# A two-layer hybrid block on one core: new orders at five seams, a tail that ends in additions, and first weights by Vector and Scalar's queue

## The chip, the cores and the metric

The kernel runs on one core of one Trainium2 chip. The metric is the time of one execution on the device, in microseconds. A core has a tensor engine (PE in the profile, with its weight loads as PEld), Vector (DVE), Scalar (ACT), GpSimd (POOL) and Sync (SP), which here only starts transfers. Scalar can start transfers as well (its rows are ACTq).

## The reference

A model of depth 2 takes x (512 tokens, width 1024) and a memory of 256 rows. Everything is float32.

```python
for layer in range(DEPTH):
    a = rmsnorm(h, ln_mix_pre[layer])
    mem_n = rmsnorm(mem, ln_mem[layer])
    if layer < N_A_LAYERS:
        proj = a @ w_in_a[layer]                       # u 768, v 768, q_mem 256
        main = chunked_spatial_gating(u, v, ...)       # gelu(u) * (w_s @ layernorm(gelu(v)) + b_s)
    else:
        kvf = rmsnorm(h, ln_shared) @ w_shared_kv      # keys, values, forget gates
        proj = a @ w_in_b[layer - N_A_LAYERS]
        main = forgetting_attention(q, k_s, v_s, log_f_s)   # 12 heads, causal, with decay
    mixed = concatenate([main, memory_attention(q_mem, mem_n, w_mem_kv[layer])])   # 4 memory heads
    h = h + rmsnorm(mixed @ w_out[layer], ln_mix_post[layer])
    f = rmsnorm(h, ln_ffn_pre[layer])
    f = (silu(f @ w_gate) * (f @ w_up)) @ w_down       # hidden width 2816
    h = h + rmsnorm(f, ln_ffn_post[layer])
```

## The kernel before

**Numbers.** Each float32 operand is kept as two parts: `hi`, a rounded copy made by Scalar, and `lo`, the rest, made by Vector (`split`, line 238). A product is three matmuls, hi·hi, hi·lo and lo·hi (`mm3`, line 180). So each weight tile of 128x1024 is loaded by Sync into a `raw` tile (four of them), cast by Scalar, subtracted by Vector, and multiplied by PE.

**Order of the work.** The program is traced in the order of the text, with work placed by hand: `attend` (line 520) runs the heads one after the other in fixed steps and calls pieces of other work (`between`) at five places of each head, so that PE has something to do while a softmax is under way. A last pass, with no new head, finishes the one before. A scheduler then makes each engine's own order, from what it takes each instruction to last and from the place in the text; `behind(x)` makes the instructions of its block come after `x` on the engine of `x`.

**Stages that the change touches.**
- *Start* (`layer_a`, lines 555 to 615). `tokens(k)` loads block k of x (256 KB) on Sync's queue and makes its scaled parts `ahi` (Scalar) and `alo` (Vector); `first_value_weights(n)` and `query_weights(m, half)` load half tiles of weights. `first_values(k)` multiplies four token blocks with the first value weights, three matmuls for each token block in turn. At the very beginning eleven matmuls on zeros (line 85) keep PE busy.
- *End of layer A's memory attention* (lines 710 to 789). Behind the last exponential, Scalar takes the gelu of six value tiles `vg` (line 716). `stats` and `normed` are the layer norm over them, `gate_inputs(m)` makes six gates u, each of 24 matmuls 512 wide, into PSUM tiles of the tag `mm`, which `spatial(g)` uses too (three tiles to a tag).
- *Tail of a projection* (`tail_of`, line 792). `tail(tb)` finishes the product of one token block, adds it to `ys`, takes the sum of squares on Scalar, and scales by r = 1/rms, which GpSimd computes (`rsqrt`, line 251).
- *Boundary* (`boundary`, line 884), three times. PE transposes the scaled token blocks, Vector adds them to the residual h, and the next projection's inputs `xs` are made by quarters (`turn`). The first half of the tokens starts with three token blocks finished; the fourth is still in `tail(3)`. Then r of the new norm is spread over the partitions by PE (`rb`, `spread`), and the sums of the first group are evacuated (`evac`).
- *Feed-forward* (`feed_forward`, line 1063). Products by blocks with seven multiplications in place of eight (`Seven`, line 973), then the down projection by groups of hidden tiles.
- *Layer B* (line 1151). `logarithms` (line 1264) makes the forget gates, with a table load on Scalar.
- *The end* (lines 1373 to 1396). `give` transposes a finished token block back, multiplies by the last gain and adds to h (`residual`, line 850), and stores. For the last block two of the eight tiles go by Scalar and GpSimd, and the last store is on Scalar's queue.

Of the kernel before, what the change touches and what calls it, by code (L numbers as in the profile page):

```python
# [15 lines left out]
P = 128  # L16
T = 512
D = 1024
KT = 8
# [23 lines left out]
def hybrid(ctx: ExitStack, tc: tile.TileContext, i: dict, out: bass.AP):  # L43
# [10 lines left out]
    last_load, last_exp, last_split = [None], [None], [None]  # L54
# [183 lines left out]
    def split(src, hi, lo, eng=None):  # L238
        last_split[0] = A.copy(hi, src), (eng or V).tensor_sub(lo, src, hi)  # L239

    def scaled_parts(src, g, hi, lo):

        A.activation(hi, src, AF.Copy, scale=g)
        V.scalar_tensor_tensor(out=lo, in0=src, scalar=g, in1=hi, op0=ALU.mult, op1=ALU.subtract)
# [174 lines left out]
    class Softmax:  # L419
# [21 lines left out]
        def turn(self, n, pieces):  # L441
# [6 lines left out]
            split(tr[:, :w], hi[:, :w], lo[:, :w])  # L448
            self.tr[n] = hi, lo
# [105 lines left out]
    def layer_a():  # L555
# [5 lines left out]
        def some_weights(raw, src, half, parts, w):  # L561
# [4 lines left out]
            split(raw[:, c], *pair)  # L566
            parts.extend(cut(pair, w))

        def query_weights(m, half):
            some_weights(raws[m], i["w_a_q"][m], half, wq[m], P)  # L570

        def first_value_weights(n):
            some_weights(raws[2 + n // 2], i["w_a_v"][0, n // 2], n % 2, w0, 256)
# [65 lines left out]
        with tc.tile_pool(name="sgu", bufs=1) as lp:  # L639
# [69 lines left out]

            between = {n: take(fill, 3) for n in range(4)}  # L710
            between[1].append(spatial_parts)
            between[3].append(spatial_bias)
            attend(mem_heads(0, q, mixed), between=between)
            with tc.issue_after(last_exp[0].ins):
                for vt in vg.values():
                    A.activation(vt, vt, AF.Gelu_apprx_tanh)
            us, vp = [], {}
            mv = lp.tile([P, TB, 2], F32, name="mv")
            rv = small("rv")

            wu = []

            def gate_inputs(m):
                while len(wu) < min(m + 2, NG):
                    wu.append(prepared(i["w_a_u"][len(wu)], (KT, P)))
                [o] = group([wu[m]], a, FULL, ["mm"])
                us.append(plain("u"))
                V.tensor_mul(us[m], o, rbc)
                A.activation(us[m], us[m], AF.Gelu_apprx_tanh)

            def stats():
# [6 lines left out]
                rsqrt(rv, rv, 4)  # L738

# [718 lines left out]
```

## Time and profile before

| what | us |
|---|---|
| median of 3 runs | 1118.45 (1118.04 to 1118.76) |
| the profiled execution, its own time | 1119.31 |
| its span, first to last instruction | 1117.6 |
| PE busy | 1101.9 |
| DVE busy | 896.5 |
| ACT busy | 659.7 |
| POOL busy | 26.3 |
| PE's mean granted clock | 0.998 of full |

A row of the order of time gives the start in us, the duration in us, the engine, the line of the kernel, the operation, its output and inputs, the shape, how many such instructions were merged (x2), and in brackets the idle time of the engine ahead of it with what ended it. A row of the waits gives the waiting engine and line, what it waited for, the total in us, how many times, and the longest. An engine's idle time costs something only where the end of the program hangs on it; here PE is nearly always that engine.

### The profile page before, as it was taken

The numbers are of one execution on the slowest core, as the hardware profiler recorded it, in microseconds if no ns is written. First come the engines' busy times: TensorE is split into PE (matmuls) and PEld (weight loads), VectorE is DVE, ScalarE is ACT, GpSimd is POOL, SyncE is SP. The second block draws the span as 40 slices with busy tenths as digits, with TensorE's granted clock in tenths as the row PEclk, the third lists the DMA queues.
The fourth block names the chain that finished last, engine by engine and source line by source line (L and its number), as shares of the span: only waits on it lengthen the run. The fifth ranks groups of instructions, "written<-read, shape, count | busy, mean of one in ns | idle before, by whom it ended". The sixth has DMA issues, their size and how long they took to land.

```text
span 1117.6 us, 19481 instructions
## 1 busy us (share of the span) xinstructions
PE 1101.9 (99%) x7374; PEld 999.6 (89%) x7374; DVE 896.5 (80%) x1739; ACT 659.7 (59%) x1391; POOL 26.3 (2%) x44
## 2 busy tenths in 40 slices
PE   9999999999999999999999999999999999999997
PEld 7987889999899899998988898889998899899996
DVE  7888658997697697886987798858898697687875
ACT  8784468665266254477666677768665266255454
POOL 0100000000000000001000000000000000000001
PEclk9999999999999999999999999999999999999999
DMA  7512222324232333244222654421223333233222
GB/s 265 161 57 95 94 77 71 118 89 142 73 114 95 105 102 114 78 150 133 91 84 74 174 127 106 145 76 57 79 93 121 106 98 111 95 106 112 85 76 76
DMA packets 64422, 118.13 MB, mean 106 GB/s; under 512 B 5260, under 2 KB 40088, under 8 KB 64328
## 3 DMA queue, kind: packets, MB, share of 16 engines
q1 hardware_dynamic: 63720, 116.18, 33.2%
q8 instruction: 58, 0.95, 0.3%
q0 software_dynamic: 192, 0.52, 0.2%
q14 instruction: 36, 0.29, 0.1%
q10 hardware_dynamic: 416, 0.18, 0.1%
HBM read 104.71 MB, written 2.10 MB: 96 GB/s over the span
## 4 chain that ended last, share of the span: by engine, by line
PE 83%; DVE 8%; ACT 4%; issue 2%; DMA 2%; POOL 1%; SPq 0%; POOLq 0%; DVEq 0%; ACTq 0%
PE y L182 9%; PE y L183 9%; PE y L184 9%; PE a L182 4%; PE a L183 4%; PE a L184 4%; PE x L184 3%; PE x L182 3%; PE x L183 3%; PE e L182 3%; PE e L184 3%; PE e L183 3%; DVE wlo L239 2%; PE ps L182 2%; PE ps L184 2%
## 5 line engine op out<-in xcount | busy, mean ns | idle before, releaser
L239 ACT CAST whi<-raw 128x512 fp32r<-128x512 f32 x460 | 275.0, 620 | 249.4 <-PE y L184 85.2
L239 DVE TENSOR_TENSOR wlo<-raw,whi 128x512 fp32r<-128x512 f32 x460 | 305.0, 690 | 74.3 <-ACT whi L239 72.5
L182 PE MATMUL y<-whi,fhi 128*128 128x512 f32 (+1 forms) x356 | 140.1, 394 | 1.2 <-DVE s L1035 1.2
L183 PE MATMUL y<-wlo,fhi 128*128 128x512 f32 (+1 forms) x356 | 139.3, 391 | 0.0
L184 PE MATMUL y<-whi,flo 128*128 128x512 f32 (+1 forms) x356 | 139.3, 391 | 0.0
L184 PE MATMUL x<-xshi,wlo 128*128 128x256 f32 x320 | 89.9, 281 | 0.0
L182 PE MATMUL a<-xshi,whi 128*128 128x256 f32 x320 | 89.8, 281 | 0.0
L183 PE MATMUL x<-xslo,whi 128*128 128x256 f32 x320 | 89.7, 280 | 0.0
L182 PE MATMUL x<-xshi,whi 128*128 128x256 f32 x320 | 89.7, 280 | 0.0
L183 PE MATMUL a<-xslo,whi 128*128 128x256 f32 x320 | 89.7, 280 | 0.0
L184 PE MATMUL a<-xshi,wlo 128*128 128x256 f32 x320 | 89.6, 280 | 0.0
L182 PEld LDWEIGHTS y<-whi,fhi 128*128 128x128 f32 x356 | 66.8, 188 | 16.8 <-DVE s L1035 2.0
L184 PEld LDWEIGHTS y<-whi,flo 128*128 128x128 f32 x356 | 66.8, 188 | 15.7 <-DVE flo L239 0.2
L183 PEld LDWEIGHTS y<-wlo,fhi 128*128 128x128 f32 x356 | 66.9, 188 | 14.8 <-DVE wlo L239 0.2
L182 PEld LDWEIGHTS a<-xshi,whi 128*128 128x128 f32 x320 | 60.2, 188 | 0.5
L183 PEld LDWEIGHTS a<-xslo,whi 128*128 128x128 f32 x320 | 60.2, 188 | 0.3
L184 PEld LDWEIGHTS x<-xshi,wlo 128*128 128x128 f32 x320 | 60.3, 188 | 0.0
L183 PEld LDWEIGHTS x<-xslo,whi 128*128 128x128 f32 x320 | 60.2, 188 | 0.0
L184 PEld LDWEIGHTS a<-xshi,wlo 128*128 128x128 f32 x320 | 60.2, 188 | 0.0
L182 PEld LDWEIGHTS x<-xshi,whi 128*128 128x128 f32 x320 | 60.2, 188 | 0.0
L182 PE MATMUL ps<-xshi,whi 128*128 128x256 f32 x192 | 53.7, 287 | 2.1 <-ACT xshi L239 2.1
L184 PE MATMUL ps<-xshi,wlo 128*128 128x256 f32 x192 | 54.2, 285 | 0.4 <-DVE wlo L239 0.4
(290 smaller groups left out, 3113.3 us busy)
## 6 DMA issues: line engine op xcount, KB each, us to landing
raw<-in_w_gate SPq DMA_DIRECT2D x44, 512.0 KB, 3.5
raw<-in_w_up SPq DMA_DIRECT2D x44, 512.0 KB, 3.5
raw<-in_w_down SPq DMA_DIRECT2D x44, 512.0 KB, 3.7
raw<-in_w_out SPq DMA_DIRECT2D x16, 512.0 KB, 4.2
raw<-in_w_b_q SPq DMA_DIRECT2D x8, 512.0 KB, 3.4
raw<-in_w_a_u SPq DMA_DIRECT2D x6, 512.0 KB
raw<-in_w_v SPq DMA_DIRECT2D x6, 512.0 KB, 3.8
raw<-in_w_k SPq DMA_DIRECT2D x6, 512.0 KB
```

Source lines behind the costliest of these rows:

```text
L182: PE.matmul(o, w[0], x[0], start=start, stop=False, skip_group_check=more)
L183: PE.matmul(o, w[0], x[1], start=False, stop=False, skip_group_check=more)
L184: return PE.matmul(o, w[1], x[0], start=False, stop=stop, skip_group_check=more)
L239: last_split[0] = A.copy(hi, src), (eng or V).tensor_sub(lo, src, hi)
```

## The change

It has eleven parts.

1. The first value weights and the first query weights are started on Scalar's queue, and the first value weights' `hi` is copied by Vector.
2. `first_values` goes by product (hi·hi for all four token blocks, then lo·hi, then hi·lo) instead of by token block.
3. The first gate's 24 matmuls become eight pieces in the last pass of layer A's attention. The other gates use the PSUM tag `lg`.
4. The gelus of `vg` come behind the last exponential and the last cast of transposed probabilities.
5. In `normed`, every second token block is normalised by Scalar (Identity with scale and bias, for which `nb` is made).
6. In `tail(3)` at a boundary, the last quarter of `xs` comes ahead of the scaling of the fourth token block.
7. At a boundary, r is spread and the first sums are evacuated after two steps of the following group.
8. Down weights are cast behind the copy of the last block's right sum on Scalar too, and not only split behind the last sum on Vector.
9. The logarithms move from the last head to the pass after it.
10. During the last feed-forward, PE turns the last gains into rows (eight transposes, two copies). In the last `tail(3)`, the sums are multiplied by them.
11. So for the last token block `give` only adds, 256 columns at a time, and nothing goes by Scalar and GpSimd. The block before it is given in the middle of the last `tail`.

```diff
-    def split(src, hi, lo, eng=None):
-        last_split[0] = A.copy(hi, src), (eng or V).tensor_sub(lo, src, hi)
+    def split(src, hi, lo, eng=None, copy=None):
+        last_hi[0] = (copy or A.copy)(hi, src)
+        last_split[0] = last_hi[0], (eng or V).tensor_sub(lo, src, hi)
...
-            last_load[0] = nc.sync.dma_start(raw[:, c], src[:, c])
+            last_load[0] = by.dma_start(raw[:, c], src[:, c])
...
+            some_weights(raws[m], i["w_a_q"][m], half, wq[m], P, by=nc.sync if m or half else nc.scalar)
...
+            some_weights(raws[2 + n // 2], i["w_a_v"][0, n // 2], n % 2, w0, 256,
+                         *(() if n else (V.tensor_copy, nc.scalar)))
...
-            for tk in range(TB):
-                c = slice(tk * P, (tk + 1) * P)
-                mm3(first_sums[tk // 2][:, tk % 2, :], (a[k][0][:, c], a[k][1][:, c]), w0[k],
-                    k == 0 and tk % 2 == 0, k == KT - 1, True)
+            for n, (x, y) in enumerate(((0, 0), (1, 0), (0, 1))):
+                for tk in range(TB):
+                    PE.matmul(first_sums[tk // 2][:, tk % 2, :], a[k][x][:, tk * P : (tk + 1) * P], w0[k][y],
...
+            def gate_piece(k):
+                if k == 0:
+                    gate_weights(1)
+                    gate.append(ps("mm"))
+                mm3(gate[0], wu[0][k], a[k], k == 0, k == KT - 1)
+
+            def gate_inputs(m):
+                gate_weights(m + 2)
+                [o] = group([wu[m]], a, FULL, ["lg"]) if m else gate
...
+            between[4] = [lambda k=k: gate_piece(k) for k in range(KT)]
             attend(mem_heads(0, q, mixed), between=between)
-            with tc.issue_after(last_exp[0].ins):
+            with behind(last_exp[0], last_turn[0]):
                 for vt in vg.values():
                     A.activation(vt, vt, AF.Gelu_apprx_tanh)
...
+                        if n:
+                            A.activation(vt[:, n, :], vt[:, n, :], AF.Identity, bias=nb[:, tk : tk + 1],
+                                         scale=rv[:, tk : tk + 1])
...
+                if final:
+                    V.tensor_mul(with_gain[dh][:, cols], y, gain_rows[dh][:, cols])
...
-            for y in ys[tb]:
-                A.activation(y, y, AF.Copy, scale=r[:, c])
+            with behind(*(ahead() if ahead else ())):
+                for y in ys[tb]:
+                    A.activation(y, y, AF.Copy, scale=r[:, c])
...
-        tail(3, lambda: turn(0, (2,)))
-        turn(0, (3,))
+        tail(3, lambda: turn(0, (2,)), lambda: turn(0, (3,)))
...
-        nnorm.spread(h0, dst)
-        evac(outs, h0)
-        outs = group(ws[:2], inputs(1), h0, ["mm", "lg"])
+
+        def evacuate(outs=outs):
+            nnorm.spread(h0, dst)
+            evac(outs, h0)
+
+        outs = group(ws[:2], inputs(1), h0, ["mm", "lg"], after={1: evacuate})
...
-                A.copy(s1[:, right], self.p)
+                last_sum[0] = A.copy(s1[:, right], self.p)
...
-            last_sum[0] = V.tensor_add(s1, self.x, s1)
+            last_sum[1] = V.tensor_add(s1, self.x, s1)
...
-                    with behind(*last_sum[: dh + kp]):
+                    with behind(*(last_sum if dh + kp else ())):
...
-                   2: take(fill, 4), 3: take(fill, 4) + [logarithms], 4: take(fill, 4)}
+                   2: take(fill, 4), 3: take(fill, 4), 4: take(fill, 3) + [logarithms] + take(fill, 1)}
...
+            for m in range(4):
+                PE.transpose(o[:, m * P : (m + 1) * P],
+                             gain(G_FFN_POST + 1, 4 * dh + m).to_broadcast([P, P]), ident)
+            gain_rows.append(plain("gr"))
+            A.copy(gain_rows[dh], o)
...
+            if final:
+                to = h[:, k0:k1, c]
+                V.tensor_add(to, tr[:, : (k1 - k0) * P].rearrange("p (a b) -> p a b", b=P), to)
...
     for tb in range(TB):
-        tail(tb)
-        if tb:
-            give(tb - 1, (range(4), range(4, 8)))
-    give(TB - 1, (range(4, 6), range(2), range(6, 8), range(2, 4)), (nc.sync,) * 3 + (nc.scalar,), (2, 3))
+        parts = iter((range(4), range(4, 8)))
+        done = lambda: give(tb - 1, (next(parts),))
+        tail(tb, done if tb == TB - 1 else None)
+        for some in parts if tb else ():
+            give(tb - 1, (some,))
+    give(TB - 1, (range(4, 6), range(2), range(6, 8), range(2, 4)), True)
```

More of the change, by code (lines that the diff above doesn't have):

```diff
@@ L708, in spatial_bias, with gate_weights @@
                                                op0=ALU.mult, op1=ALU.add)
+            us, vp = [], {}
+            mv = lp.tile([P, TB, 2], F32, name="mv")
+            rv, nb = small("rv"), small("nb")
+            wu = []
+            gate = []
+            def gate_weights(n):
+                while len(wu) < min(n, NG):
+                    wu.append(prepared(i["w_a_u"][len(wu)], (KT, P)))
+            def gate_piece(k):
[6 more added lines that the diff above has]
+                [o] = group([wu[m]], a, FULL, ["lg"]) if m else gate
+                us.append(plain("u"))
+                V.tensor_mul(us[m], o, rbc)
+                A.activation(us[m], us[m], AF.Gelu_apprx_tanh)
             between = {n: take(fill, 3) for n in range(4)}
@@ L799, in tail_of, with tail @@
         ss, v, r = small("ss", 12), small("v"), small("r")
-        def tail(tb, halfway=None):
+        def tail(tb, halfway=None, ahead=None):
             if not ws:
@@ L809, in tail @@
             two = small("two", 1) if final else None
+            with_gain = [temp("yg") for _ in range(2)] if final else None
             at = [(0, 0, 4), (1, 0, 2), (1, 2, 4)] if final else [(0, 0, 4), (1, 0, 4)]
@@ L1364, in memory, with end_gains @@
         yield
+    gain_rows = []
+    def end_gains():
+        yield
+        for dh in range(2):
+            o = ps("tr", s="gr")
+            for m in range(4):
[3 more added lines that the diff above has]
+            A.copy(gain_rows[dh], o)
+        yield
     with tc.tile_pool(name="ffn0", bufs=4) as xp:
@@ L1370, in hybrid, with give @@
     with tc.tile_pool(name="ffn1", bufs=4) as xp:
-        tail, ys, _ = feed_forward(1, phase, xp)
-    def give(tb, order, queues=(nc.sync,), aside=()):
-        c = (tb * P, (tb + 1) * P)
+        tail, ys, _ = feed_forward(1, phase, xp, end_gains())
+    def give(tb, order, final=False):
+        c = slice(tb * P, (tb + 1) * P)
         for n, some in enumerate(order):
```

53 lines of the change are left out of this document (21 added, 32 removed).

## The prediction

> **What bounds the kernel now.** I read the page first, then the table by stage, then the list of what the tensor engine (PE) waited for, then the order of time around each wait.
>
> ```profile
> span 1117.6 us, 19481 instructions
> PE 1101.9 (99%) x7374; PEld 999.6 (89%) x7374; DVE 896.5 (80%) x1739; ACT 659.7 (59%) x1391; POOL 26.3 (2%) x44
> ```
>
> PE is busy for 99% of the span: only 1117.6 - 1101.9 = 15.7 us are idle. Three rows of the table by stage (stretch, length, then busy us and instructions of PE, its weight loads, DVE, ACT and POOL):
>
> ```profile
> 84.00:112.00 28.00, 26.95 (x126) 22.07 (x125) 25.04 (x55) 12.87 (x23) 1.31 (x1) 1.00 0.30 95
> 224.00:252.00 28.00, 28.00 (x240) 28.00 (x239) 28.00 (x51) 18.73 (x40) 0.00 (x0) 1.00 0.29 95
> 364.00:392.00 28.00, 28.00 (x123) 22.64 (x121) 17.33 (x28) 6.21 (x10) 0.00 (x0) 1.00 0.36 113
> ```
>
> The last two give PE's pace where nothing stalls: 28.00/240 = 0.117 us for a matmul 256 wide, 28.00/123 = 0.228 for one 512 wide. (A row lasts longer than its slot, because matmuls overlap, so the idle time shown is 0.1 to 0.2 us short of the real stall.) PE's waits, in us in total, times, longest:
>
> ```profile
> PE ps L182 <- ACT xshi L239: 2.1, 2, 1.1
> PE yt L848 <- DVE y L837: 2.0, 1, 2.0
> PE mo L475 <- ACT pT L239: 1.5, 2, 1.2
> PE y L182 <- DVE s L1035: 1.2, 1, 1.2
> PE ps L182 <- DVE u L728: 1.0, 1, 1.0
> PE rb L249 <- POOL r L252: 0.7, 3, 0.2
> PE ps L183 <- DVE xslo L239: 0.5, 2, 0.3
> PE ps L184 <- DVE wlo L239: 0.4, 1, 0.4
> ```
>
> They are few and stand at seams between stages. The change cuts no matmul of the model; it can win only such waits, at the head and the tail too. Without the tail's 2.0 the list comes to 7.4 us: that is the size of what can be had at the seams.
>
> **The change part by part.** I go by seams in order of time. One thing holds for all: an engine's order is not that of the text (line 105 is traced ahead of all activations of the input, yet its row below starts at 10.11), so an edit can move more than itself.
>
> *Start.*
>
> ```profile
> 4.34 0.72 ACT L243 ACTIVATE ahi<-h,gains 128x512 fp32r<-128x512 f32 x1 [1.60 <-DMA gains<-in_gains]
> 4.97 0.60 ACT L239 CAST whi<-raw 128x512 fp32r<-128x512 f32 x1
> 5.62 0.93 PE L182 MATMUL v<-whi,ahi 128*128 128x256 f32 x2
> 7.09 0.28 PE L182 MATMUL v<-whi,ahi 128*128 128x256 f32 x1
> 8.68 0.72 ACT L243 ACTIVATE ahi<-h,gains 128x512 fp32r<-128x512 f32 x1 [1.89 <-DMA h<-in_x]
> 9.44 0.75 DVE L244 SCALAR_TENSOR_TENSOR alo<-h,gains,ahi 128x512 fp32r<-128x512 f32 x1 [1.73 <-ACT ahi L243]
> 10.11 0.22 DVE L105 CAST ident_b<-ident 128x128 bf16<-128x128 f32 x1
> 31.32 0.16 DVE L282 TENSOR_SCALAR var<-st 128x2 f32<-128x2 f32 x1
> ```
>
> PE's first product waits for the cast that follows ahi on ACT and ends at 5.57. On Vector the cast runs beside ahi. The trace has no such copy; bounds are 0.22 (a quarter of the width) and 0.60 (the same cast on ACT), and I take 0.45. The first product could start at 5.06, when ahi ends, if the weights are there. They were by 4.97; on Scalar's queue they share the DMA engines with h's second block, and may come 0.7 us later. In the new order (four high products, four with alo, four with wlo) wlo is needed 7 matmuls later than before. By itself this is worth 0 to 0.9 us. But Vector works without a break from 9.44 until var at 31.32, and from var follow r and the first transposes of rb, for which PE waits already. So PE keeps only what Vector gains, and that hangs on h's third block, used at 8.68: it is issued earlier now, with as many bytes around it. I take -0.2, bounds -1.2 and +0.5.
> The Trainium skill ("DMA: Bandwidth & Descriptors", section "Issuing engines are not separate DMA queues") says that transfers begun by several engines run on the same DMA engines, so that only issue time is saved; by that rule alone this term is 0.0. Nothing in this trace tells the two apart, since only the small gains go by Scalar's queue there.
>
> *End of the first attention, and the gates.*
>
> ```profile
> 77.88 1.66 ACT L716 ACTIVATE vg<-vg 128x512 f32<-128x512 f32 x3
> 79.44 0.57 ACT L239 CAST pT<-tr 128x512 fp32r<-128x512 f32 x1
> 80.06 0.50 PE L475 MATMUL mo<-pT,memv 128*128 128x512 f32 x1 [1.17 <-ACT pT L239]
> 98.64 0.69 DVE L728 TENSOR_TENSOR u<-ps,rbc 128x512 f32<-128x512 f32 x1
> 99.38 0.50 PE L182 MATMUL ps<-ahi,whi 128*128 128x512 f32 x1 [1.05 <-DVE u L728]
> ```
>
> Gelus stand ahead of the cast of pT, for which PE waits 1.17. Now they stand behind it, and eight gate pieces (24 x 0.228 = 5.5 us of work that came afterwards) lie around the transposes and value products: the wait goes. What is late next: the gelus, by some 2 us, and the second gate's weights cast after them; I charge 0.2. Term -1.0, bounds -1.6 and +1.5. Half of the normalisation goes to ACT, idle for 15 of the 28 us from 84 to 112; its Identity appears nowhere in the trace, and I price it at under 0.6 by the gelus (1.66/3) of twice its width, hidden. The 1.05 at 99.38 is a PSUM tile that gate 2 holds until Vector has multiplied it; in the other tag the fourth gate has a free tile. Term -1.0, bounds -1.2 and 0.
>
> *Boundaries.*
>
> ```profile
> 171.12 1.33 ACT L841 ACTIVATE y<-y,r 128x512 f32<-128x512 f32 x2 [0.31 <-POOL r L252]
> 172.36 0.60 ACT L239 CAST xshi<-hs 128x512 fp32r<-128x512 f32 x1
> 173.01 0.50 PE L182 MATMUL ps<-xshi,whi 128*128 128x256 f32 x2 [1.06 <-ACT xshi L239]
> 176.23 1.03 PE L848 MATMUL yt<-ident,y 128*128 128x128 f32 x8
> ```
>
> ACT scales the fourth token block (1.33) while PE waits for the cast behind it. With the cast first, it ends at 171.7 instead of 172.96. Two boundaries have this (2.1 in two waits) and a wait for xslo behind it (0.5 in two); I take 2 x (1.05 + 0.15). What is late next is the scaled block: the transposes at 176.23 read it, and it is ready at about 173.1, so the cover is 3 us. Spreading r behind 12 matmuls (1.4 us) takes away the waits for it at the seams: -0.5 of the 0.7. The PSUM tiles that evacuation frees come 1.4 us later; the cover is the first block of the last group, 24 x 0.117 = 2.8 us. The middle boundary's 0.4 is the wait for wlo, whose cast stood behind the same scaling: -0.2. Together -3.1, bounds -4.2 and 0.
>
> *End of the second attention, down weights.*
>
> ```profile
> 602.96 1.28 ACT L1270 ACT_TABLE_LOAD   x1
> 605.02 0.50 PE L475 MATMUL mo<-pT,memv 128*128 128x512 f32 x1 [0.35 <-ACT pT L239]
> ```
>
> ```profile
> 856.50 1.14 ACT L239 CAST whi<-raw 128x512 fp32r<-128x512 f32 x2 [0.79 <-DMA raw<-in_w_down]
> 857.55 0.36 ACT L1023 COPY s<-a 128x256 f32<-128x256 f32 x1
> 858.42 0.50 PE L182 MATMUL y<-whi,fhi 128*128 128x512 f32 x1 [1.17 <-DVE s L1035]
> ```
>
> The table load for the logarithms stands ahead of the second pT; some pieces later it doesn't: -0.4, bounds -1.0 and +0.3. The copy at 857.55, which frees PE's tile, stood behind casts that waited for a transfer; casts ordered behind it cannot block it: -1.15, bounds -1.3 and 0.
>
> *Tail.*
>
> ```profile
> 1111.28 0.61 DVE L837 TENSOR_SCALAR y<-y,r 128x256 f32<-128x256 f32 x2 [0.40 <-POOL r L252]
> 1111.81 2.14 DVE L853 SCALAR_TENSOR_TENSOR h<-yt,gains,h 128x128 f32<-128x128 f32 x7
> 1114.27 0.40 ACTq L1390 DMA_DIRECT2D out<-h  x1
> ```
>
> Turning the gains into rows adds eight transposes in a stage where PE is full. The eight at 176.23 took 1.03, some 0.2 of it overlap: +0.8. After the last r nothing changes until the transposes. Then four additions 256 wide end the work, where seven steps 128 wide (2.14/7 = 0.31 each) and two on POOL did. An addition is bounded by 0.31 and 0.61, and I take 0.4: they end at about 1113.5, and the last transfer starts then instead of at 1114.27: -0.7. Multiplying by the gains adds 0.7 and twice 0.4 on Vector (0.69 for 512 wide, as u at 98.64); the last lies beside the square, and for the others, queued ahead of the last sum, I give back 0.2. Together +0.3, bounds -0.9 and +1.3.
>
> **Sum:** -0.2 - 1.0 - 1.0 - 3.1 - 0.4 - 1.15 + 0.3 = -6.55 us. The profiled execution took 1119.31 (its span and 1.7 around it); the median of the runs shown is 1118.45, 0.86 less, and the gain is taken from that: **1111.9 us**.
>
> **The rivals.**
> *Half comes back.* A stall removed uncovers the next one: Vector is at 80% over the span and at 25.04 of 28 around the gates, so r, wlo and xslo may be what PE waits for next. Against it: long stages follow where PE is busy for all of its 28 us, and they swallow what the others are late. With half of the seams' 6.65 and the rest as above, -3.2: 1115.2.
> *No difference.* The new orders only move the waits, and the gain rows' 0.8 is paid: 1118.5, within 0.2% (2.2 us, about what a measurement of this kernel can tell from no change).
> *Slower: the first weights stand behind ahi on Scalar's queue.* In the text the transfer comes after the activation that waits until 4.34. The issue takes 0.4 (as at 1114.27), and the landing of such a transfer, issues by line with size and median us to landing:
>
> ```profile
> raw<-in_w_a_v SPq DMA_DIRECT2D x4, 256.0 KB, 5.4
> ```
>
> Behind ahi, PE starts at 5.06 + 0.4 + 5.4 = 10.9 instead of 5.62: 5.2 later. After an idle gap of some 4 us it may also run at half pace anew: its first two matmuls took 0.93, four slots of 0.117 each, and full pace came at 7.09. Half of 7.09, 3.5 us, bounds that loss; with 2.8 the price is 8. 1118.45 - 6.35 + 8 = 1120.1, and with a quarter of the seams' gain lost 1121.8. It decides from 6.35 us of delay on. For it: the order of the text. Against it: line 105 shows that what waits for nothing need not keep that order, and ACT's queue has nothing else to do before 4.34.
>
> **How the numbers follow.** Forecast 0.60, half 0.18, no difference 0.09, slower 0.13. The forecast and most of half lie over 2.2 us under the time before: faster 0.75, within 0.2% 0.12, slower 0.13. The forecast's own range is 1109 to 1114.5. The range reaches down to 1107.8 (the start at its bound, and half of what the seams' bounds leave) and up to 1119.5, over the no-difference case; the slower case is left out.
>
> **What would show it.** In the list of PE's waits, xshi, mo, u, s of line 1035 and r should be gone or under 0.2 us each time. The first product should start between 5.1 and 6.2; later than 8 is the slower rival. The last transfer should start 2.3 us after the scaling by r does, instead of 3.0. The forecast is wrong if new waits at these seams come to over 3 us, above all between 80 and 98 us (gelus late) or before 34 us (Vector still full).

## The result and the profile after

| | us |
|---|---|
| before, median of 14 runs beside the kernel after | 1118.58 (1117.87 to 1119.36) |
| after, median of 14 runs | 1117.47 (1115.27 to 1118.76) |
| ratio after to before, 95% interval | 0.999 (0.9982 to 0.9998) |
| forecast | 1111.9 (1107.8 to 1119.5) |

The change gains 1.1 us where 6.55 were forecast. The time lies in the range, the forecast does not hold. The head of the page after:

```profile
span 1116.3 us, 19503 instructions
PE 1104.4 (99%) x7382; PEld 1003.7 (90%) x7382; DVE 894.6 (80%) x1736; ACT 660.1 (59%) x1396; POOL 25.3 (2%) x42
```

PE's waits after (engine and line, what it waited for, us in total, times, longest):

```profile
PE yt L873 <- DVE yg L860: 2.3, 1, 2.3
PE idle L85 <- DVE idle L82: 1.3, 1, 1.3
PE ps L182 <- ACT whi L239: 1.2, 1, 1.2
PE v L586 <- DVE whi L239: 1.0, 1, 1.0
PE ps L183 <- DVE xslo L240: 0.6, 2, 0.3
PE rb L250 <- POOL r L253: 0.5, 2, 0.2
PE y L182 <- DVE y L840: 0.4, 1, 0.4
```

Set beside the list of before: the waits for xshi, mo, u and the s of line 1035 (2.1, 1.5, 1.0 and 1.2) are gone, as forecast. Two new ones stand at the start, 1.2 and 1.0, and one of 0.4 in the tail. But the waits do not show the whole loss, since a PE at half pace counts as busy. For that one goes by the start of the same instruction in both traces, here called a mark. The first product of the statistics (`st`) is such a mark, since all of the start lies ahead of it. In before:

```profile
29.08 0.95 PE L280 MATMUL st<-avg,acc 128*128 128x1 f32 x8
```

And in after:

```profile
33.71 0.95 PE L281 MATMUL st<-avg,acc 128*128 128x1 f32 x8
```

The start is 4.63 us **later**; from there to the end of the span (1117.6 and 1116.3) the kernel after gains 5.9. The order of time at the start of the kernel after, PE, DVE and ACT mixed by time:

```profile
1.24 0.46 ACTq L566 DMA_DIRECT2D raw<-in_w_a_v  x1
1.73 0.45 ACTq L566 DMA_DIRECT2D raw<-in_w_a_q  x1
6.59 0.43 DVE L239 CAST whi<-raw 128x512 fp32r<-128x512 f32 x1 [4.28 <-DMA raw<-in_w_a_v]
7.16 1.19 PE L586 MATMUL v<-whi,ahi 128*128 128x256 f32 x4 [1.03 <-DVE whi L239]
8.92 0.62 ACT L239 CAST whi<-raw 128x512 fp32r<-128x512 f32 x1 [4.06 <-DMA raw<-in_w_a_q]
9.45 0.72 ACT L244 ACTIVATE ahi<-h,gains 128x512 fp32r<-128x512 f32 x1
9.59 0.79 PE L182 MATMUL ps<-ahi,whi 128*128 128x512 f32 x1 [1.24 <-ACT whi L239]
10.18 1.05 PE L586 MATMUL v<-whi,alo 128*128 128x256 f32 x4
11.04 1.05 PE L586 MATMUL v<-wlo,ahi 128*128 128x256 f32 x4
13.60 0.87 PE L586 MATMUL v<-wlo,ahi 128*128 128x256 f32 x4
14.30 0.39 PE L183 MATMUL ps<-alo,whi 128*128 128x512 f32 x1
```

Three things are to be seen. First, both transfers are issued at once (1.24 and 1.73), not behind `ahi`: the slower rival's mechanism did not occur. But the value weights are there only at 6.59, where before they had been by 4.97. Second, the cast of the query weights waits for its transfer until 8.92, and ACT takes what stands behind it, the second `ahi`, only at 9.45; PE has one query product ahead of the products with `alo` and waits for the same cast. Third, PE's pace: four products take (11.04 - 10.18)/4 = 0.21 us each, against 0.117 at full pace; it is half until about 14.1, before it was until 7.09. The record of the granted clock in the two traces fits: its first entry, full clock, stands at 14.10 and at 7.07. (Ahead of that entry the view by stretch gives 1.00 as well, for 10 to 14 us too, so the pace of the start has to be read from the spacing of the products.)

The experiments first take the start apart, then price the seams and the tail. In each, the times of before are from the same chip and session (medians 1118.45 to 1118.92). Differences between two experiments are differences of their medians, though some are from different chips; set against the before of its own session, such a difference moves by up to 0.5.

### The profile page after: what moved, and what is told of

The parts are those of the page before. It is cut to its first block, busy times and chain, and to the rows that moved or that the text cites. A ratio compares the mean times of both kernels' runs of the same rounds, so it can differ in the third digit from the quotient of the medians.

```text
span 1116.3 us, 19503 instructions
## 1 busy us (share of the span) xinstructions
PE 1104.4 (99%) x7382; PEld 1003.7 (90%) x7382; DVE 894.6 (80%) x1736; ACT 660.1 (59%) x1396; POOL 25.3 (2%) x42
## 4 chain that ended last, share of the span: by engine, by line
PE 94%; ACT 2%; DVE 1%; issue 1%; DMA 1%; POOL 0%; ACTq 0%; POOLq 0%; DVEq 0%
PE y L182 10%; PE y L183 9%; PE y L184 9%; PE a L182 5%; PE a L184 5%; PE a L183 5%; PE x L184 3%; PE e L182 3%; PE e L184 3%; PE e L183 3%; PE x L182 3%; PE x L183 3%; PE ps L184 3%; PE ps L182 3%; PE ps L183 3%; PE tr L447 2%
## 5 line engine op out<-in xcount | busy, mean ns | idle before, releaser
L183 PE MATMUL ps<-xslo,whi 128*128 128x256 f32 x192 | 53.8, 283 | 0.6 <-DVE xslo L240 0.6
```

The costliest lines, as they stand in the source:

```text
L183: PE.matmul(o, w[0], x[1], start=False, stop=False, skip_group_check=more)
```

## The experiments

**Both transfers back on Sync's queue** (e1_sync): the kernel after with

```diff
-            some_weights(raws[m], i["w_a_q"][m], half, wq[m], P, by=nc.sync if m or half else nc.scalar)
+            some_weights(raws[m], i["w_a_q"][m], half, wq[m], P)
...
-                         *(() if n else (V.tensor_copy, nc.scalar)))
+                         *(() if n else (V.tensor_copy,)))
```

> The change with both first transfers of weights back on Sync's queue; everything else of it stays. Theory Q (the transfers on Scalar's queue cost the start some 4.5 us: the weights land later, and Scalar and PE are ordered for an early landing that does not come): the first product at 5.1 to 6.2 us, full pace near 7 us, the whole 5 to 7 us faster than the kernel before (1111.5 to 1113.5). Rival O (the Vector copy and the new product order cost the start): the first product still after 6.5 us, the whole within 2 us of the changed kernel (1115.5 to 1118.5).

Measured: 1113.94 (1113.65 to 1114.98), ratio 0.9959 (0.9946 to 0.9971). Its start:

```profile
4.98 0.43 DVE L239 CAST whi<-raw 128x512 fp32r<-128x512 f32 x1 [2.67 <-DMA raw<-in_w_a_v]
5.55 0.78 PE L586 MATMUL v<-whi,ahi 128*128 128x256 f32 x4
6.96 0.62 ACT L239 CAST whi<-raw 128x512 fp32r<-128x512 f32 x1 [0.60 <-DMA raw<-in_w_a_q]
7.43 0.64 PE L586 MATMUL v<-wlo,ahi 128*128 128x256 f32 x4
28.92 0.95 PE L281 MATMUL st<-avg,acc 128*128 128x1 f32 x8
```

With the copy on Vector and the new order of products still in, `st` stands at 28.92, 0.16 ahead of before. That this is the forecast's -0.2 is in part luck: five more traces with the same start, of experiments further down (e6, e7, e8, e10, e11), have `st` at 29.02 to 29.55. The whole loss, 1117.47 - 1113.94 = 3.5 us (3.9 with each set against its own before), belongs to the two transfers on Scalar's queue. Each landed later there though it was issued earlier or as early: the value weights at 6.59 instead of 4.98, the query weights, issued at 1.73, at 8.92 instead of 6.96. These two traces are the extremes for the value weights. Over all traces their cast starts at 5.57 to 6.59 with Scalar's queue (six) and, where Vector casts, at 4.98 to 5.61 with Sync's (eight); the query weights' cast starts at 8.08 to 9.23 with Scalar's (five) and at 6.44 to 7.43 with Sync's (nine of the kernels with the change).

**Only the value weights on Scalar's queue** (e2_values_only), the first of the two edits above alone.

> The change with only the first value weights on Scalar's queue; the query weights are back on Sync's, and with that the orders of Scalar and PE are those without an early landing. Theory Q: the weights land about 1.5 us later than on Sync's queue (copy at some 6.3 us), but neither the second token block nor the second products wait for the query weights: 3 to 5.5 us faster than the kernel before. Rival O: as the changed kernel, 0 to 2 us faster. If the late landing alone were the whole cost, 0 to 2 us faster as well.

Measured: 1114.27 (1113.08 to 1114.77), ratio 0.9957 (0.9944 to 0.9969). Vector's copy starts at 5.85, the first product at 6.43, `st` at 29.81. So the later landing of the value weights costs 0.9 at `st` (0.3 against the latest of the traces above) and, by the medians, 0.3 of the time, which is within the spread of the runs. The rest comes with the query weights' transfer.

**The kernel before with the two transfers on Scalar's queue** (e3_before_scalar), and nothing else of the change:

```diff
-            last_load[0] = nc.sync.dma_start(raw[:, c], src[:, c])
+            last_load[0] = by.dma_start(raw[:, c], src[:, c])
```

> The kernel before with the two first transfers of weights on Scalar's queue and nothing else of the change; its orders on Scalar, Vector and PE stay those of before. Theory Q: the cast of the first value weights waits until some 6.6 us, the first product starts at about 7.2 instead of 5.6, and the whole is 1.5 to 4 us slower than the kernel before, by whether full pace comes late too. Rival O: no change within 0.5 us.

Measured: 1120.08 (1119.24 to 1121.37), ratio 1.0012 (1.0003 to 1.0021): a loss of 1.2, `st` at 29.74, 0.66 late. Here the engines' orders stay those of before until both tiles are cast; further on Scalar's and Vector's moved as well (the first sum of squares, `acc`, at 12.47 instead of 9.31). The transfers without the change cost about a microsecond; the rest of the kernel after's 3.5 needs its orders as well.

**More zero matmuls** (e4_fillers): the kernel after with 14 instead of 11 at line 84.

> The changed kernel with 14 instead of 11 matmuls on zeros at the beginning, so that PE is busy until the first product at some 7.2 us. Rival G (the loss is PE's half pace, which lasted until 14.1 us because PE stood idle from 6.1 to 7.2): full pace comes between 7 and 8 us, and 2.5 to 3.5 us come back. Theory Q: the wait for the query weights from 8.4 to 9.6 us stays, and at most 2 us come back, by an earlier full pace.

Measured: 1115.28 (1114.43 to 1115.7), ratio 0.9967 (0.9954 to 0.9979): 2.2 of the 3.5 come back. PE is at full pace from its second four products on (0.74 for them, at 7.65); `st` stands at 31.45. But the scheduler also put the query product behind the other first products, so this run alone doesn't separate pace from PE's order. ACT's order was as in the kernel after.

**The cast behind the second `ahi`** (e5_cast_behind): both transfers stay on Scalar's queue; only ACT's order is held.

```diff
             pair = pair_of_parts()
-            split(raw[:, c], *pair, copy=copy)
+            with behind(*first):
+                split(raw[:, c], *pair, copy=copy)
...
+                         first=() if m or half else (last_hi[0],))
```

> The kernel after, with both first transfers still on Scalar's queue, but the cast of the first query weights ordered behind the scaling of h's second block on ACT (the order that the kernels with one transfer or none there have). If the orders that come from an early landing of the query weights cost the time (first theory): the four high products and the four with alo run without the query product between them, PE is at full pace before 9 us, the first statistics product starts at 29.8 to 31.0 (33.7 in the kernel after) and the time is 1114.3 to 1115.5. If the second transfer itself costs it, by its share of the DMA engines (rival): h's second block and the value weights land as late as in the kernel after, the first statistics product stays at 33 or later, and the time at 1116.8 to 1117.8.

Measured: 1113.91 (1113.82 to 1114.36), ratio 0.9959 (0.9944 to 0.9974).

```profile
5.70 0.70 ACT L244 ACTIVATE ahi<-h,gains 128x512 fp32r<-128x512 f32 x1
5.93 0.43 DVE L239 CAST whi<-raw 128x512 fp32r<-128x512 f32 x1 [3.62 <-DMA raw<-in_w_a_v]
6.50 0.71 PE L588 MATMUL v<-whi,ahi 128*128 128x256 f32 x4 [0.88 <-ACT ahi L244]
8.08 0.62 ACT L239 CAST whi<-raw 128x512 fp32r<-128x512 f32 x1 [1.67 <-DMA raw<-in_w_a_q]
29.87 0.95 PE L281 MATMUL st<-avg,acc 128*128 128x1 f32 x8
```

One ordering edge takes all of it back: the time is that of e1_sync. The weights still land a microsecond late, but the second `ahi` is made at 5.70 and not at 9.45, PE has work, and it is at full pace from 6.50 on (0.71 for four). At `st` 29.87 - 28.92 = 0.95 of the loss is left, 0.3 against the latest trace with Sync's queue. The two traces meet again only near 1050 us, with the same matmuls in between, so a shift of up to about 0.9 between two single traces tells nothing by itself. The rival, that the second transfer's share of the DMA engines costs the time, falls.

**The cast ahead, with all transfers on Sync's queue** (e9_cast_ahead), the counterpart, on e1_sync:

```diff
-        tokens(1)
-        first_values(1)
-        query_weights(0, 0)
+        tokens(1, lambda: query_weights(0, 0))
+        first_values(1)
```

> The counterpart: all transfers on Sync's queue (1113.9 with the usual orders), but the cast of the first query weights ordered ahead of the scaling of h's second block on ACT, as in the kernel after. If the place of this cast is a cost by itself (first theory): the second block's products wait until the query weights have landed and been cast, PE waits 1 us or more for ahi there, the first statistics product starts at 30.3 to 32 (28.92 with the usual order), and the time is 1115.0 to 1116.5; where PE's gap also keeps it at half pace, up to 1117.5. If it costs only together with transfers on Scalar's queue (rival): 28.9 to 29.5, and 1113.7 to 1114.5.

Measured: 1114.66 (1113.87 to 1115.12), ratio 0.9966 (0.9952 to 0.9979). The mark came out as the rival has it, the time just above its column. The cast starts at 6.72 without a wait for its transfer, PE does not wait for `ahi`, and `st` stands at 29.26. A cast ahead of the second `ahi` costs little by itself (0.7 by the medians, with ranges that overlap; 1.2 with each set against its own before); it costs where its transfer lands late, at 8.92 instead of by 6.72. The most of the loss needs **both**, the late landing and an order that supposes an early one.

**PE kept busy over the gap** (e12_keep_pace): the kernel after with six zero matmuls behind the four high products; PE's query product moves behind the other first products with it.

```diff
                               skip_group_check=True)
+                if (k, n) == (0, 0):
+                    z = ps("tr", s="idle")
+                    for _ in range(6):
+                        PE.matmul(z, idle[:, :P], idle, start=True, stop=True)
```

> The kernel after, with the orders on ACT as they are (query weights' cast ahead of the scaling of h's second block) and both first transfers on Scalar's queue, but six zero matmuls on PE behind the four high products, and the query product thereby behind the other first products. If the half pace until 14.1 makes most of the loss (first theory): PE is at full pace before 11, the first statistics product starts at 30.8 to 32.2 (33.71 in the kernel after), and the time is 1114.6 to 1115.6. If the late products make it (rival): PE stays busy with zeros, the rest comes as late, 33 or later, and the time is 1116.5 to 1117.8.

Measured: 1115.73 (1114.83 to 1116.28), ratio 0.9972 (0.9962 to 0.9982).

```profile
8.57 0.64 PE L586 MATMUL v<-wlo,ahi 128*128 128x256 f32 x4
9.23 0.62 ACT L239 CAST whi<-raw 128x512 fp32r<-128x512 f32 x1 [4.00 <-DMA raw<-in_w_a_q]
9.75 0.72 ACT L244 ACTIVATE ahi<-h,gains 128x512 fp32r<-128x512 f32 x1
10.53 0.74 PE L586 MATMUL v<-whi,ahi 128*128 128x256 f32 x4 [1.32 <-ACT ahi L244]
31.95 0.95 PE L281 MATMUL st<-avg,acc 128*128 128x1 f32 x8
```

ACT is as late as in the kernel after, and PE waits 1.32 for `ahi`, but at full pace (0.64 and 0.74 for four). Pace, together with the new place of the query product, is worth 1117.47 - 1115.73 = 1.7 of the 3.5; the other 1115.73 - 1113.94 = 1.8 is late landing and late cast. This trace can't part the two causes of the 1.7: the value weights were cast at 5.57 in it, full clock was granted at 6.34, and PE did not idle ahead of its first product.

**Fewer zero matmuls without Scalar's queue** (e13_few_fillers): e1_sync with 5 instead of 11.

> The kernel after with both transfers on Sync's queue (1113.9) and 5 instead of 11 zero matmuls at the start, so that PE idles ahead of its first product for some 2 us; nothing else is changed, all weights land and are cast as early as before. If PE's pace follows from how busy it was (first theory): the first products run at half pace, full pace comes 3 to 7 later than with 11, the first statistics product starts 1.5 to 3.5 after 28.92, and the time is 1115.0 to 1117.4. If the pace doesn't hang on the zero matmuls (rival): the first products take 0.78 for four, and the time is 1113.7 to 1114.5.

Measured: 1116.3 (1115.81 to 1116.73), ratio 0.9977 (0.9967 to 0.9986).

```profile
5.87 1.20 PE L586 MATMUL v<-whi,ahi 128*128 128x256 f32 x4 [2.30 <-DVE whi L239]
10.75 1.05 PE L586 MATMUL v<-wlo,ahi 128*128 128x256 f32 x4
12.35 0.40 PE L184 MATMUL ps<-ahi,wlo 128*128 128x512 f32 x1
```

Half pace until about 12.2 (the first entry of the granted clock is at 12.21) with everything else early costs 2.4 us, with `st` at 31.48. So a PE that has idled for 2.3 us ahead of its first products loses as much as the late landing and the late cast do. The two prices of e12 (1.7 and 1.8) add to the whole because they are differences over the same run; e13 shows apart from it that half pace alone costs as much and needs no late weights.

**The boundaries of before** (e8_old_boundaries), on e1_sync:

```diff
-        tail(3, lambda: turn(0, (2,)), lambda: turn(0, (3,)))
+        tail(3, lambda: turn(0, (2,)))
+        turn(0, (3,))
...
-        outs = group(ws[:2], inputs(1), h0, ["mm", "lg"], after={1: evacuate})
+        nnorm.spread(h0, dst)
+        evac(outs, h0)
+        outs = group(ws[:2], inputs(1), h0, ["mm", "lg"])
```

> The kernel after with both transfers on Sync's queue (1113.9), with the boundaries of before: the fourth token block is scaled ahead of the cast of xshi, r is spread and the tiles are evacuated ahead of the next group. By the prediction's term (3.1): 1117.0. By the landmarks of the kernel with both transfers on Sync's queue (0.7 at the first, 0.6 at the middle and 0.7 at the third boundary): 1115.9, and between 1115.5 and 1116.3. The waits for xshi come back with about 1.0 each.

Measured: 1115.92 (1115.4 to 1116.59), ratio 0.9974 (0.9964 to 0.9983). The wait is back in full:

```profile
PE ps L182 <- ACT xshi L239: 2.1, 2, 1.1
```

So the boundaries are worth 1115.92 - 1113.94 = 2.0, not 3.1. What is late next, in e1_sync at the first boundary:

```profile
168.06 0.60 ACT L239 CAST xshi<-hs 128x512 fp32r<-128x512 f32 x1
168.19 0.69 DVE L310 TENSOR_TENSOR sq<-sq,sq 128x512 f32<-128x512 f32 x1 [0.90 <-ACT sq L308]
168.72 0.50 PE L182 MATMUL ps<-xshi,whi 128*128 128x256 f32 x2
168.80 0.69 DVE L240 TENSOR_TENSOR xslo<-hs,xshi 128x512 fp32r<-128x512 f32 x1
169.54 0.39 PE L183 MATMUL ps<-xslo,whi 128*128 128x256 f32 x1 [0.32 <-DVE xslo L240]
```

PE no longer waits for xshi, but Vector takes a sum of squares ahead of xslo, and PE waits 0.32 for that (before 0.23). From the same transposes (166.99 in before) to the down projection's first product (195.62) e1_sync gains 0.71, at the third boundary 0.73, with the same matmuls in between.

**The tail of before** (e6_old_tail), on e1_sync: no rows of gains, no products with them, residual steps 128 wide, the third block given behind the last sums, as the minus lines of parts 10 and 11 of the change have it.

> The kernel after with both transfers on Sync's queue (1113.9) and with the tail of before: no rows of gains, no products with them, steps of residuals 128 wide, the output of the third block behind the last sums. If the tail's parts cost what the landmarks say (rows of gains 0.9, the last sums 0.85, the end after the last transposes 0.0): 1112.2, that is 1111.8 to 1112.7. If the tail is worth what the prediction took (rows +0.8, sums +0.2, the end -0.7): 1113.6. If the work of Vector that was put ahead of the last sums only changes its place: 1113.0.

Measured: 1113.59 (1113.0 to 1113.9), ratio 0.9955 (0.994 to 0.9969): 0.35 ahead of e1_sync. That fits the prediction's +0.3, but the runs of each spread over 0.9 to 1.3, so it can't be told from no difference.

**Only the third block's output behind the last sums again** (e7_give_behind), on e1_sync:

```diff
-        tail(tb, done if tb == TB - 1 else None)
-        for some in parts if tb else ():
-            give(tb - 1, (some,))
+        tail(tb)
+        if tb:
+            give(tb - 1, (range(4), range(4, 8)))
```

> The kernel after with both transfers on Sync's queue (1113.9), with only one edit in the tail undone: the third block's output stands behind the last block's sums again. If Vector's residual steps and products with the gains, queued ahead of the last sums, hold the last sums by 0.85: 1113.1. If they then stand between the last sums and the last transposes instead: 1113.9 or more, to 1114.5. With 0.9 for the rows of gains still in it, it stays 0.8 to 1.0 behind the kernel with the old tail by the first, 1.5 or more by the second.

Measured: 1114.19 (1113.47 to 1114.74), ratio 0.9958 (0.9944 to 0.9972): no gain, the second answer. From the start of the last down projection (1084.33 in before) to the last transposes it loses 0.1 against before, where e1_sync loses 0.85. The span then ends 6.9 after the start of those transposes (1105.61 to 1112.5) instead of 5.9: Vector still has residual steps of the third block there, and the transposes ran at half pace (1.92 for the eight, 1.09 in e1_sync), so the order alone isn't priced by this run.

**Narrow last additions** (e10_narrow_adds): e1_sync with eight additions 128 wide in place of four.

```diff
-                to = h[:, k0:k1, c]
-                V.tensor_add(to, tr[:, : (k1 - k0) * P].rearrange("p (a b) -> p a b", b=P), to)
+                for x, k in enumerate(some):
+                    to = h[:, k, c]
+                    V.tensor_add(to, tr[:, x * P : (x + 1) * P], to)
```

> The kernel after with both transfers on Sync's queue (1113.9), with the last additions 128 wide, eight instead of four, so that Vector's last work takes some 2.0 instead of 1.42. If the last 512 KB of output set the end, which flow for 2.0 from the first final transfer on (first theory): the last issue comes 0.3 to 0.6 later than 2.34 after the scaling by r, but the last data end 4.2 to 4.5 after that scaling, as they did (1105.85 to 1110.2), and the time is 1113.7 to 1114.3. If the last addition sets the end (rival): the span's end moves with the last issue, and the time is 1114.4 to 1114.7.

Measured: 1114.23 (1113.73 to 1114.78), ratio 0.9963 (0.9949 to 0.9976). The eight took 1.68, the last issue came at 1108.20, 2.59 after the scaling by r (1105.61) instead of 2.34, and the span ended at 1112.0, 6.4 after that scaling, as in e1_sync. The issue moved 0.25 and the end did not; the medians, 0.3 apart with ranges of a microsecond, are too close to settle it.

**The better version** (e11_best): e6_old_tail with the third block's output between the last sums, the loop of the kernel after.

> The version to be tried as the better one: the kernel with both transfers on Sync's queue and the old tail (1113.6), but with the third block's output between the last block's sums, as in the kernel after; no rows of gains, no products with them. If the products with the gains are what holds the last sums on Vector: the last sums lose 0.3 or less, 256 KB of output are gone before the end, and the time is 1112.8 to 1113.4. If the residual steps between the sums hold them as much as before: 1113.5 to 1114.1.

Measured: 1113.48 (1113.14 to 1113.68), ratio 0.9955 (0.9941 to 0.9968), just outside the first answer: 0.1 from e6_old_tail, no difference that can be told. It beats both kernels: by 5.0 us the one before in the same session (1118.45), by 4.0 the one after (1117.47). But e1_sync, too, lies 5.0 ahead of its own before; all that is shown to pay is the two transfers back on Sync's queue, or the one ordering edge.

## Why the prediction was wrong

**The start** is the step that failed: "I take -0.2, bounds -1.2 and +0.5". It lost 4.6 at `st`, and by the medians the two transfers alone cost 3.5. The prediction priced the first product's earlier cast, and of the transfers only that the value weights "may come 0.7 us later". Three things were missing.

*The landing.* The sum had the value weights' lateness as a bound and the query weights' not at all. The view of the transfers in the first 12 us (packets, MB, mean rate; then Scalar's queue, q10, with its share of the DMA engines), after:

```profile
DMA packets 1954, 3.36 MB, mean 280 GB/s; under 512 B 339, under 2 KB 339, under 8 KB 1954
q10 hardware_dynamic: 432, 0.57, 14.7%
```

The same view of e1_sync:

```profile
DMA packets 2009, 3.45 MB, mean 288 GB/s; under 512 B 347, under 2 KB 347, under 8 KB 2009
q10 hardware_dynamic: 144, 0.05, 2.2%
```

The engines move no more bytes with two queues, 3.36 against 3.45 MB; here the second queue only changed which bytes came first. On one queue the first weights stood second and fourth; on their own queue it appears that they share with everything on Sync's. The prediction cited the Trainium skill ("DMA: Bandwidth & Descriptors", section "Issuing engines are not separate DMA queues") for a term of 0.0 by saved issue time alone. The traces agree with its other half, that such transfers interleave on the same engines, and that half was the one that mattered: 1.6 later for the first tile and 2.0 for the second, between e1_sync and after. For the first tile the 0.7 of the prediction is nearer to the usual: the middles of the two ranges above, 5.57 to 6.59 and 4.98 to 5.61, are 0.8 apart. The second tile, which it left out, is the one with the price.

*The order.* The prediction used line 105 as proof that an engine's order isn't that of the text, so that an edit "can move more than itself", but worked out no such move on ACT. With both transfers on Scalar's queue the query weights' cast stood ahead of the second `ahi`, and h's second block, which e5_cast_behind could scale at 5.70, waited until 9.45 for weights that it doesn't need. Holding the cast behind that `ahi`, and nothing else, gives 1113.91. It appears that the scheduler took the transfer to land early; what it reckons isn't in a trace, so this reading of its motive is argued, and only the order and its price are shown.

*The pace.* The price of half pace was in the prediction, at 3.5 as a bound, but only inside the slower rival, "behind ahi". It belonged to every case in which PE may idle among its first products before it has full pace. In the kernel after it idled for 1.03 and 1.24 and was at half pace until 14.1. In e5_cast_behind it idled for 0.88 ahead of the first product and was at full pace from there on; full clock had been granted at 4.97, ahead of that gap. Whether a gap meets PE before or after the grant is partly chance: with the same eleven zero matmuls the grant came at 3.89 to 7.07 in twelve traces, and at 14.10 in that of the kernel after. Half pace cost 2.4 by itself (e13_few_fillers), and 1.7 went with it in e12_keep_pace, where PE's order changed too. The 14 runs of the kernel after fit this. The two shortest, 1115.27 and 1115.5, lie at the times of e4_fillers and e12_keep_pace; the other twelve are 1117.04 to 1118.76, and seven of these have a mean granted clock of 0.994 to 0.996, below every other run on record (0.997 to 1.0). The mean does not show all of it, since it counts nothing ahead of the first grant: e13_few_fillers has 0.997 to 0.999. No trace of the two short runs was kept. The Trainium skill ("TensorE: Matmul & The Clock Gate", section "Part 1: The HAM clock gate (the "warmup" mystery)") says that full rate is granted after a busy window of some 3.4 us, in windows that run on by themselves. By that, as an estimate, full pace comes 3.4 to 6.8 after PE is busy for good; in e13_few_fillers it came about 6.3 after (5.87 to 12.2), in the kernel after 4.5 (9.59 to 14.1). The traces agree.

**The seams** were right in kind. Shifts of marks in e1_sync, which has all of the change but the queue, against before:

| term | forecast | e1_sync |
|---|---|---|
| start without the queue | -0.2 | -0.2 |
| end of the first attention and gates | -2.0 | -3.2 |
| three boundaries | -3.1 | -2.0 |
| end of the second attention | -0.4 | -0.8 |
| down weights | -1.15 | -1.4 |
| tail | +0.3 | +1.7 |
| sum to the span's end | -6.55 | -5.4 (1117.6 to 1112.2) |

The terms sum to -5.9; they leave out a slip of -0.4 near 830 us and slow drifts (from 870 to 1084 us the shift falls from -7.77 to -7.06 with no edit in between). By medians it is 5.0 (1118.92 to 1113.94). That the sum comes within 1.6 of the forecast is in part luck: the gates gave 1.2 more, the boundaries 1.1 less, and the tail cost 1.4 more, beyond its bound of +1.3. Nor does the range's lower end follow from the bounds as it says: the start at its bound is 1.0, and half of what the seams' bounds leave (9.3 against 6.65) is 1.3, together 1109.6 and not 1107.8. *Boundaries*: some 0.5 of each 1.2 stayed in what came next, xslo behind a sum of squares on Vector, as the rival "half comes back" had it. The -0.5 for r did not come: r is still waited for (0.7 in three waits in e1_sync and in before). *Gates* gave more: with a wait of 1.17 and one of 1.05 taken as the whole price, the smaller slips around them were left out. *Down weights* were right to 0.3, with the wait for s gone.

*Tail*: the rows of gains cost 0.8 (+0.8 forecast; the last mark ahead of them, 1084.21 in before, shifts by -7.06, the first behind them, 1084.33, by -6.27). From there to the last transposes (1111.68 in before, 1106.26 in e1_sync) another 0.85 goes, where 0.2 was given back: on Vector a product with the gains and residual steps of the third block stand ahead of the addition that frees PE's tile, and the last transposes of the third block no longer lie under the wait for r. In e7_give_behind, with those steps behind the last sums, 0.1 of the 0.85 is left there. And the -0.7 at the end didn't come, though the step that was to bring it worked. In e1_sync:

```profile
1077.26 1.04 PE L1402 MATMUL gr<-ident,gains 128*128 128x128 f32 x8
1102.25 0.38 PE L182 MATMUL y<-whi,fhi 128*128 128x256 f32 x1 [0.45 <-DVE y L840]
1105.85 0.62 DVE L860 TENSOR_SCALAR yg<-yg,r 128x256 f32<-128x256 f32 x2 [0.66 <-POOL r L253]
1106.74 1.42 DVE L1426 TENSOR_TENSOR h<-yt,h 128x256 f32<-128x256 f32 x4 [0.27 <-PE yt L873]
1108.19 0.46 ACTq L1430 DMA_DIRECT2D out<-h  x1
```

The last transfer starts 1108.19 - 1105.85 = 2.34 after the scaling, the forecast's 2.3 (before 3.0). But the span ends 4.0 after it, where it ended 3.3 after it in before. Where that goes shows in the transfers over the last 8.0 us of the span, in 40 slices of 0.2 us, in before:

```profile
GB/s 3 261 287 292 287 182 0 0 0 0 0 0 41 0 0 0 0 120 300 271 310 279 269 305 284 261 290 279 305 279 292 90 0 0 0 0 0 0 0 0
```

In e1_sync:

```profile
GB/s 0 0 164 302 287 289 251 18 0 0 0 0 0 0 0 0 0 0 0 128 292 218 261 259 190 302 289 279 289 116 0 0 0 0 0 0 0 0 0 0
```

The output flows without a pause, mostly at 250 to 300 GB/s, through 15 slices in before (256 KB of the third block among it) and 11 in e1_sync, and 1.6 to 2.0 us after the flow the span ends. In e1_sync the last 512 KB flow for about 2.1 us. That the flow and not the last addition sets the end fits e10_narrow_adds, but is not settled by it. Against the old tail the sum fits, as far as the runs can tell: +0.35 by the medians (e6_old_tail), +0.3 forecast. By marks the new one is 0.8 dearer, since the old one, too, loses 0.9 in e6_old_tail, where the last eight transposes took 1.70 and not 1.21 as in before.

**The rivals.** "No difference" (1118.5, a chance of 0.09) came nearest in time, but by luck: the seams did gain, and the start lost it again. "Slower" had the right place, Scalar's queue at the start, and the right second price, the pace, but a mechanism that did not occur: 1.24 and 1.73 are the issues.

**The signs named ahead.** xshi, mo, u and s gone: right. r: wrong. First product between 5.1 and 6.2: 7.16, wrong, though short of the 8 that was to mark the slower rival. Last transfer 2.3 after the scaling: 1112.53 - 1109.66 = 2.87 in the kernel after, where the last transposes ran at half pace, and 2.34 in e1_sync. New waits before 34 us over 3 us: 2.3 in waits, 4.6 at `st`; the sign was set on waits and missed the pace.

## What to carry to other kernels

A second queue added no bandwidth here: when the first tile is urgent, keep it in front of the one queue that is full anyway, and ask for every tile moved what then lands later. After an edit that moves a transfer, read each engine's order for a step that waits for it with something urgent behind; one ordering edge may be worth more than the transfer. Price a gap ahead of or among the first matmuls twice, as its length and as the half pace that may follow it, and look for the latter in the spacing of matmuls, since no list of waits shows it. Before a reading rests on one trace, look at how far the same mark moves between traces with the same start.

## What the runs showed of the hardware

- An activation queue's transfer issued at 1.73 was used at 8.92, when it had landed; the same bytes issued 0.46 later as fourth on Sync's queue (2.19, in e9_cast_ahead) were cast at 6.72.
- Half pace at the end, too: after the same wait of 2.3 us the last eight transposes took 1.97 in the kernel after and 1.09 in e1_sync:

```profile
1110.07 1.97 PE L873 MATMUL yt<-ident,yg 128*128 128x128 f32 x8 [2.32 <-DVE yg L860]
1106.26 1.09 PE L873 MATMUL yt<-ident,yg 128*128 128x128 f32 x8 [2.33 <-DVE yg L860]
```

  The granted clock was 0.50 from 1110 to 1112 in the first and 0.99 from 1106 to 1108 in the second. So an idle stretch of 2.3 can be enough to lose the pace, and need not be.
- The grant of full clock at the start moves between traces: 3.89 to 7.07 in twelve traces with the same eleven zero matmuls.
- The copy of a 128x512 tile to the rounded type takes 0.43 on Vector (0.45 was assumed), against 0.60 to 0.62 on Scalar in the same part of the kernel; an addition 256 wide at the end 1.42/4 = 0.36 (0.4 assumed).
